# Other homes for the working tiles of an RWKV merge

## Chip, cores and metric

One core of a Trainium2 chip. The metric is the time of one execution on the device, in microseconds (us), as the median of several runs. The engines are TensorE (PE; its weight loads are listed as PEld), VectorE (DVE), ScalarE (ACT), GpSimd (POOL) and SyncE (SP), which issues the DMAs.

## The reference

Two layers of a diffusion backbone over 256 context and 256 latent tokens of 1024 channels. A layer is a half-step SwiGLU, a token mixing of three branches (retention, windowed attention, RWKV-7), and another half-step SwiGLU, all in float32. The change is in the RWKV branch, a recurrence over tokens in both directions, for 8 heads of 64 channels:

```python
# S_t = S_{t-1} (diag(w_t) - kk_t^T (a_t * kk_t)) + v_t^T k_t ;  y_t = S_t r_t
def step(S, inp):
    r_t, w_t, k_t, a_t, v_t, kk_t = inp
    sa = -jnp.einsum('bhvk,bhk->bhv', S, kk_t)
    S = (S * w_t[:, :, None, :] + sa[..., None] * (kk_t * a_t)[:, :, None, :]
         + v_t[..., None] * k_t[:, :, None, :])
    return S, jnp.einsum('bhvk,bhk->bhv', S, r_t)
...
ys_f, S_f = rwkv7_scan(r_s, *dirs_s[0], v_s, kk_s, zero_rw, False)
ys_b, S_b = rwkv7_scan(r_s, *dirs_s[1], v_s, kk_s, zero_rw, True)
yx_f, _ = rwkv7_scan(r_x, *dirs_x[0], v_x, kk_x, S_f, False)
yx_b, _ = rwkv7_scan(r_x, *dirs_x[1], v_x, kk_x, S_b, True)
```

The latent scans (x) start from the final state of the context scans (s). The second layer's output is wanted for the latent tokens alone.

## The kernel before

Channels lie on the 128 partitions, the 512 tokens (256 context, 256 latent) along the free dimension. Every dense product is three float32r matmuls (L186 to L188): the weights are loaded in blocks of four 128x128 tiles, ScalarE rounds them (L114) and VectorE takes the rest (L115).

In a mixing stage the string ORDER[l] gives the order in which the work of the branches is written down, by hand. The final order on each engine is made from it by a planner at build time, which runs a model of the machine with durations of its own, lets instructions whose inputs and buffers are there go ahead of others, and keeps in force how many tiles of each tag may be alive. A tile is asked for with mk(shape, tag, bufs): tiles of one tag share bufs homes, and a tile waits until one of them has been released by its last reader. PSUM banks are asked for with ps(tag); the tag "rx" has two.

RWKV is done for four pairs of heads p, and for the two streams, context (s = 0) and latent (s = 1), in chunks of 64 tokens. In ORDER, "A" and "C" are the fronts of context and latent, "B" and "D" their backs; "lo" makes the inputs of the low-rank products, "c" the columns of a pair.

- The front, rw_prep (L902 on), makes the decays, the keys and the products inside a chunk, with eight tiles of the tag "rt", and has GpSimd invert triangular blocks of 32 (L1008, L1009). The inverses go to the HBM tile td.
- The back is rw_merge, rw_vals, rw_chain and, where the output is wanted, rw_out. rw_merge loads the inverses (z, L1018), copies them into tg (L1026, L1027), transposes half of them into tn (L1023), and joins the blocks of 32 to blocks of 64 by two groups of small matmuls (L1035, L1040) with the copy xm (L1036) between them. rw_vals puts the values into ve, the tile in which the chain later replaces half of the rows by corrected values (L1088), and into the block-diagonal vbd (L1060). rw_chain goes through four chunks in both directions, 8 steps of some six short operations each, which wait for each other on TensorE, ScalarE and VectorE (L1079 to L1113); its result ya and the squares of rw_out take "rb" tiles.

Before the change tn, xm, ya and the squares share three homes of "rb"; ve has two homes, one for each direction; vbd is one lasting buffer, a slice of the constant tile cst; the "lo" inputs have three homes.

Of the kernel before, what the change touches and what calls it, by code (L numbers as in the profile page):

```python
# [18 lines left out]
CONSTS = {"ident": 0, "nw": 128, "adab": 176, "ones": 320, "bones": 384, "cm": 512, "mg": 640, "ks": 896, "all": 960}  # L19
# [103 lines left out]
def body(nc, tc, I, O, es, dbg=None):  # L123
# [3 lines left out]
    V, A, G, PE, SP = nc.vector, nc.scalar, nc.gpsimd, nc.tensor, nc.sync  # L127

    def mk(shape, tag, bufs=1, dt=F32):
        return sb.tile(shape, dt, name=tag, tag=tag, bufs=bufs)  # L130
# [3 lines left out]
    def ps(tag):  # L134
        return pp.tile([128, 512], F32, name="ps_" + tag, tag=tag, bufs=NB[tag])
# [13 lines left out]
    def span(S):  # L149
        return slice(S[0] * 256, S[-1] * 256 + 256)  # L150


    cst = mk([128, CONSTS["all"] + 1696 + 4360], "cst")
    n0 = CONSTS["bones"]
    SP.dma_start(out=cst[:, 0:n0], in_=I["cst"][:, 0:n0])
    SP.dma_start(out=cst[:, n0:CONSTS["all"]], in_=I["cst"][:, n0:])
# [1 line left out]
    def const(name, n):  # L158
        return cst[:, CONSTS[name]:CONSTS[name] + n]
# [4 lines left out]
    per = cst[:, CONSTS["all"]:]  # L164
# [3 lines left out]
    def sm(n, key, bufs=8):  # L168

        if key not in rings:  # L170
            rings[key] = [rings["at"], 0, n]
            rings["at"] += n * bufs
            assert rings["at"] <= CONSTS["all"] + 1696 + 4360
        r = rings[key]
        assert r[2] == n
        j = r[0] + n * (r[1] % bufs)
        r[1] += 1
        return cst[:, j:j + n]
# [1 line left out]
    hall = mk([128, KT, 2, 512], "hall", 1, F32R)  # L180
    hs = [(hall[:, kt, 0], hall[:, kt, 1]) for kt in range(KT)]

    rings = {"at": CONSTS["all"] + 1696}

    def mm3(o, w, h, start, stop):
        PE.matmul(o, w[0], h[0], start=start, stop=False)  # L186
# [19 lines left out]
    st = {"apart": False}  # L206
# [120 lines left out]
    def hl(h, c):  # L327
        return h[0][:, c], h[1][:, c]
# [21 lines left out]
    def first(W, key, H, cs, os, lead=0, lag=0):  # L350

        bl, n = W.take(key), len(os)
        w = {}
        parts = [(0, slice(0, 512))] if lead == 0 else [(0, CS[0]), (lead, CS[1])]
        for i in range(KT + lead + lag):
            for d, part in parts:
                k = i - d
                for j, (o, c) in enumerate(zip(os, cs)):
                    p = slice(max(c.start, part.start), min(c.stop, part.stop))
                    if 0 <= k < KT and p.start < p.stop:  # L360
                        if (k, j) not in w:
                            w[k, j] = W.get(bl[k * n + j])
                        for q in range(2):
                            PE.matmul(o[:, p], w[k, j][q], hl(H[k], p)[0], start=(k == 0 and q == 0 and p.start == c.start), stop=False)  # L364
                k -= lag
                for j, (o, c) in enumerate(zip(os, cs)):
                    p = slice(max(c.start, part.start), min(c.stop, part.stop))
                    if 0 <= k < KT and p.start < p.stop:
                        PE.matmul(o[:, p], w[k, j][0], hl(H[k], p)[1], start=False, stop=(k == KT - 1 and p.stop == c.stop))
# [424 lines left out]
    def conv(o, ct, c, st, dst):  # L794
        w = st["vec"][:, ct * 3:ct * 3 + 3]
        A.activation(dst[:, c], o[:, c], AF.Copy, scale=w[:, 1:2])
        n = (c.stop - c.start) // 256
        d = dst[:, c].rearrange("p (s t) -> p s t", s=n)
        s = o[:, c].rearrange("p (s t) -> p s t", s=n)
        V.scalar_tensor_tensor(d[:, :, 1:256], s[:, :, 0:255], w[:, 0:1], d[:, :, 1:256], ALU.mult, ALU.add)  # L800
        V.scalar_tensor_tensor(d[:, :, 0:255], s[:, :, 1:256], w[:, 2:3], d[:, :, 0:255], ALU.mult, ALU.add)  # L801

    def rw_consts():
        V.memset(per[:, 288:1312], 0.0)
        ub = per[:, 288:800].rearrange("p (d b x) -> p d b x", d=2, b=2)
        return dict(bones=const("bones", 128), cm=const("cm", 128), mg=const("mg", 256).rearrange("p (d x) -> p d x", d=2),
                    one=const("ones", 64), ks=const("ks", 1), ub=[[ub[:, d, b] for b in range(2)] for d in range(2)],
                    vbd=per[:, 800:1312].rearrange("p (q x) -> p q x", q=4))

    def rw_lora(W, H, l, S, st):  # L810
        full = slice(0, 512)
        vec = st["vec"]
        lo = []
        cs, os = (full, full, span(S)), [ps(t) for t in ("mm", "mm", "ap")]
        first(W, "lo", H, cs, os, 1, 1)
        for j, (c, o) in enumerate(zip(cs, os)):
            t = mk([128, 512], "lo", 3)
            conv(o, 12 + j, c, st, t)
            lo.append(t)
        c = span(S)  # L820
        A.activation(lo[0], lo[0], AF.Tanh)
        A.activation(lo[2][:, c], lo[2][:, c], AF.Tanh, scale=0.5)
        V.tensor_scalar(lo[2][:, c], lo[2][:, c], 0.5, 0.5, ALU.mult, ALU.add)
        st["sg"] = lo[2]
        st["lw"] = [[mk([128, 512], "lw", 4, F32R) for d in range(2)] for x in range(2)]
        for x in range(2):
            for d in range(2):
                hs, ot = (slice(64 * y, 64 * y + 64) for y in (d, 1 - d))
                A.copy(st["lw"][x][d][hs], lo[x][hs])
                V.tensor_sub(st["lw"][x][d][ot], lo[x][hs], st["lw"][x][d][hs].bitcast(F32))  # L830
        if l > 0:
            bl = W.take("vd")
            o = ps("mm")
            wh, wl = W.get(bl[0], 2)
            for kt in range(KT):
                ksl = slice(kt * 32, kt * 32 + 32)
                mm3(o[0:32], (wh[:, ksl], wl[:, ksl]), hl(H[kt], full), kt == 0, kt == KT - 1)
            vd = mk([128, 512], "vd")[0:32]
            A.copy(vd, o[0:32])
            st["vd"] = vd  # L840
# [172 lines left out]
        X["td"] = td  # L1013

    def rw_merge(X, st):
        z, tn, xm = mk([64, 2, 8, 32], "z", 2), mk([32, 16, 32], "rb", 3)[:, 0:8], mk([64, 16, 32], "rb", 3)[:, 0:8]
        for b in range(2):
            mark = SP.dma_start(out=z[32 * b:32 * b + 32].rearrange("p d u t -> p (d u) t"), in_=X["td"][16 * b:16 * b + 16].rearrange("u j g i -> (j g) u i")).ins  # L1018
        st["marks"].append(mark)
        fl = lambda t: t.rearrange("p u t -> p (u t)")  # L1020
        tg = X["tg"]
        tu = [tg[d].rearrange("p h c t -> p (h c) t") for d in range(2)]
        V.transpose(fl(tn), fl(z[0:32, 0]))  # L1023
        for b in range(2):
            bs = slice(32 * b, 32 * b + 32)
            A.copy(tu[0][bs, :, bs], z[bs, 0])  # L1026
            V.transpose(tu[1][bs, :, bs], z[bs, 1])  # L1027

        o = ps("rx")
        ov, o2 = (o[:, j * 256:j * 256 + 256].rearrange("p (u x) -> p u x", x=32) for j in range(2))  # L1030
        ab = (slice(0, 32), slice(32, 64))
        for d in range(2):
            a, b = ab[d], ab[1 - d]
            for u in range(8):
                PE.matmul(ov[b, u], X["off"][a, u], tn[:, u] if d == 0 else z[a, 1, u], start=True, stop=True)  # L1035
        A.copy(xm, ov[0:64])  # L1036
        for d in range(2):
            a, b = ab[d], ab[1 - d]
            for u in range(8):
                PE.matmul(o2[a, u], xm[b, u], tu[d][b, u, b], start=True, stop=True)  # L1040
        V.tensor_copy(tu[0][ab[0], :, ab[1]], o2[ab[0]])
        A.copy(tu[1][ab[1], :, ab[0]], o2[ab[1]])

    def rw_vals(s, R, st, want_y, X):
        c = CS[s]
        v = R["v"]

        ve = [mk([128, 4, 128], "ve", 2) for _ in range(2)]
        vb = st["vbd"]
        o = ps("rx")  # L1050
        for q in range(2):
            PE.matmul(o[:, q * 128:q * 128 + 128], v[:, c.start + q * 128:c.start + q * 128 + 128], st["cm"], start=True, stop=True)
        ov = o[:, 0:256].rearrange("p (c d) -> p c d", c=2)
        for a in range(2):
            rows = slice(64 * a, 64 * a + 64)
            for d in range(2):
                A.copy(ve[d][0:64, a::2], ov[rows])
            for h in range(2):
                hs = slice(64 * h, 64 * h + 64)
                A.copy(vb[hs, a::2, hs], ov[rows, :, hs])  # L1060
        X["ve"], X["vb"] = ve, vb
        if want_y:
            o = ps("rx")
            PE.matmul(o[:, 0:256], st["bones"], X["t"][:, 0], start=True, stop=True)
            bv = sm(256, "bv", 2)
            V.tensor_tensor(bv, o[:, 0:256], v[:, c], ALU.mult)
            X["bv"] = bv
# [159 lines left out]
    for l in range(2):  # L1227
# [17 lines left out]
        if not RC:  # L1245
            RC.update(rw_consts())
# [120 lines left out]
```

## Time and profile before

| what | us |
|---|---|
| median of three runs | 2946.3 (2938.15 to 2952.78) |
| the profiled execution's own time | 2950.47 |
| its span, first to last instruction | 2948.7 |
| TensorE busy | 2797.0 (95%) |
| VectorE busy | 2002.5 (68%) |
| ScalarE busy | 1319.8 (45%) |
| GpSimd busy | 376.2 (13%) |

The profile comes from one execution. Its times count from the span's start. Layer 0's mixing stage lies between about 410 and 1300 us, layer 1's between about 2070 and 2750 us. The granted clock is the share of its full speed that TensorE was given; it has two levels, 1.2 and 2.4 GHz, so a mean of 0.82 in a stretch says that about a third of it was at the lower one.

### The profile page before, as it was taken

The numbers are of one execution on the slowest core, as the hardware profiler recorded it, in microseconds if no ns is written. First come the engines' busy times: TensorE is split into PE (matmuls) and PEld (weight loads), VectorE is DVE, ScalarE is ACT, GpSimd is POOL, SyncE is SP. The second block draws the span as 40 slices with busy tenths as digits, with TensorE's granted clock in tenths as the row PEclk, the third lists the DMA queues.
The fourth block names the chain that finished last, engine by engine and source line by source line (L and its number), as shares of the span: only waits on it lengthen the run. The fifth ranks groups of instructions, "written<-read, shape, count | busy, mean of one in ns | idle before, by whom it ended". The sixth has DMA issues, their size and how long they took to land. (4 is left out here: it accounts for less than half of the span.)

```text
span 2948.7 us, 47410 instructions
## 1 busy us (share of the span) xinstructions
PE 2797.0 (95%) x16761; PEld 2389.1 (81%) x16761; DVE 2002.5 (68%) x4677; ACT 1319.8 (45%) x2968; POOL 376.2 (13%) x1068
## 2 busy tenths in 40 slices
PE   7999999889999999999999999999989889899999
PEld 6888888767877787788888888888878788788999
DVE  7977668676676666566756466465787767678655
ACT  3322245556555654333223232233567665565544
POOL 0000000522132112000000000000033434330000
PEclk9999999789999999999999999999999888899999
DMA  7655534212333136534534435343433234246554
GB/s 267 232 189 183 163 122 130 83 39 82 111 97 89 49 123 207 176 102 147 195 114 169 147 111 185 104 164 122 137 90 108 75 110 116 61 124 212 170 179 154
DMA packets 259727, 400.97 MB, mean 136 GB/s; under 512 B 78752, under 2 KB 96288, under 8 KB 259488
## 3 DMA queue, kind: packets, MB, share of 16 engines
q1 hardware_dynamic: 259488, 397.93, 42.2%
q8 instruction: 132, 2.16, 0.3%
q14 instruction: 107, 0.88, 0.1%
HBM read 368.33 MB, written 25.82 MB: 134 GB/s over the span
## 5 line engine op out<-in xcount | busy, mean ns | idle before, releaser
L114 ACT CAST whi<-raw 128x512 fp32r<-128x512 f32 x954 | 564.1, 618 | 675.7 <-PE ps_mm L187 350.0
L186 PE MATMUL ps_mm<-hall,whi 128*128 128x512 f32 (+1 forms) x2320 | 845.1, 365 | 10.2 <-DVE rr_v L801 4.0
L188 PE MATMUL ps_mm<-hall,wlo 128*128 128x512 f32 (+1 forms) x2320 | 842.6, 364 | 2.0 <-DVE wlo L115 2.0
L187 PE MATMUL ps_mm<-hall,whi 128*128 128x512 f32 (+1 forms) x2320 | 840.8, 363 | 0.0
L115 DVE TENSOR_TENSOR wlo<-raw,whi 128x512 fp32r<-128x512 f32 x954 | 643.8, 691 | 104.3 <-ACT whi L114 68.3
L186 PEld LDWEIGHTS ps_mm<-hall,whi 128*128 128x128 f32 x2320 | 442.9, 191 | 80.6 <-ACT cst L981 4.4
L188 PEld LDWEIGHTS ps_mm<-hall,wlo 128*128 128x128 f32 x2320 | 441.6, 191 | 74.8 <-DVE wlo L115 4.1
L187 PEld LDWEIGHTS ps_mm<-hall,whi 128*128 128x128 f32 x2320 | 442.0, 191 | 71.4 <-issue 0.2
L186 PE MATMUL ps_mm<-hid,whi 128*128 128x512 f32 (+1 forms) x737 | 260.6, 354 | 0.0
L187 PE MATMUL ps_mm<-hid,whi 128*128 128x512 f32 (+1 forms) x737 | 259.9, 354 | 0.0
L188 PE MATMUL ps_mm<-hid,wlo 128*128 128x512 f32 (+1 forms) x737 | 257.3, 354 | 0.0
L1008 POOL TENSOR_TENSOR cst<-acc,cst 128x60 f32<-128x60 f32 (+24 forms) x496 | 172.4, 348 | 615.5 <-DMA acc<-ad__10934 59.2
L401 DVE TENSOR_TENSOR ft<-ft,ps_mm 128x512 f32<-128x512 f32 (+1 forms) x80 | 49.7, 621 | 210.4 <-PE ps_mm L188 198.1
L373 DVE SCALAR_TENSOR_TENSOR x<-ps_mm,cst,x 128x256 f32<-128x256 f32 x136 | 61.0, 480 | 193.1 <-PE ps_mm L188 193.1
L853 POOL TENSOR_TENSOR ll<-lora,lh 128x512 fp32r<-128x512 f32 x8 | 10.3, 1282 | 1359.2 <-DVE ft L300 942.6
L1009 POOL TENSOR_TENSOR cst<-cst 128x60 f32<-128x60 f32 (+24 forms) x496 | 176.2, 355 | 38.1
L236 DVE SCALAR_TENSOR_TENSOR ft<-m,cd 128x1024 bf16<-128x1024 f32 x136 | 163.0, 1221 | 9.8 <-DMA m<-ada 9.8
L237 DVE SCALAR_TENSOR_TENSOR m<-m,cd 128x1024 f32<-128x1024 f32 x136 | 165.4, 1221 | 0.7
L186 PEld LDWEIGHTS ps_mm<-hid,whi 128*128 128x128 f32 x737 | 139.1, 189 | 19.6
L187 PEld LDWEIGHTS ps_mm<-hid,whi 128*128 128x128 f32 x737 | 139.1, 189 | 19.4
L188 PEld LDWEIGHTS ps_mm<-hid,wlo 128*128 128x128 f32 x737 | 138.5, 189 | 19.4
L187 PE MATMUL ps_mm<-wlo,hall 128*128 128x256 f32 x416 | 122.6, 295 | 2.7 <-DVE wlo L115 2.6
(339 smaller groups left out, 4505.3 us busy)
## 6 DMA issues: line engine op xcount, KB each, us to landing
m<-ada SPq DMA_DIRECT2D x136, 512.0 KB, 4.4
raw<-w0b SPq DMA_DIRECT2D x214, 256.0 KB, 2.9
raw<-w1b SPq DMA_DIRECT2D x211, 256.0 KB, 3.2
raw<-w0a SPq DMA_DIRECT2D x132, 256.0 KB, 2.8
raw<-w0c SPq DMA_DIRECT2D x132, 256.0 KB, 4.5
raw<-w1a SPq DMA_DIRECT2D x132, 256.0 KB, 4.3
raw<-w1c SPq DMA_DIRECT2D x132, 256.0 KB, 3.9
gd<-ft SPq DMA_DIRECT2D x24, 256.0 KB, 2.0
```

The lines of the kernel that those rows point to most:

```text
L114: nc.scalar.copy(hi, raw)
L115: nc.vector.tensor_sub(lo, raw, hi.bitcast(F32))
L186: PE.matmul(o, w[0], h[0], start=start, stop=False)
L187: PE.matmul(o, w[0], h[1], start=False, stop=False)
L188: PE.matmul(o, w[1], h[0], start=False, stop=stop)
L236: V.scalar_tensor_tensor(junk, raw, 1.0, st["cond"][0], ALU.mult, ALU.mult, accum_out=md[:, kt, 0:1])
L237: V.scalar_tensor_tensor(raw, raw, 1.0, st["cond"][1], ALU.mult, ALU.mult, accum_out=md[:, kt, 1:2])
L373: V.scalar_tensor_tensor(xs[n][:, CS[s]], o[:, CS[s]], gate[:, n, s:s + 1], xs[n][:, CS[s]], ALU.mult, ALU.add)
L401: V.tensor_tensor(sg[:, c], sg[:, c], pu[:, c], ALU.mult)
L853: G.tensor_sub(ll, lw, lh.bitcast(F32))
L1008: G.tensor_tensor(w, acc[j // 16][:, j % 16, j + 1:32].unsqueeze(1).to_broadcast([128, m, n]), tt[:, 0:m, j:j + 1].to_broadcast([128, m, n ...
L1009: G.tensor_tensor(tt[:, 0:m, j + 1:32], tt[:, 0:m, j + 1:32], w, ALU.add)
```

## The change

The two working tiles of a merge, tn and xm, are taken from "rt" (eight homes, those of the preparation) in place of "rb" (three homes, which stay). ve gets four homes in place of two; the first two "lo" inputs, which are dead long before, use them too, and "lo" keeps one home. vbd becomes two lasting buffers, one for each stream; the tile cst is 512 columns (2 KiB a partition) wider for it, and the second buffer is set to zero once. The PSUM banks, ORDER and all computing instructions but that memset stay as they were.

```diff
-    cst = mk([128, CONSTS["all"] + 1696 + 4360], "cst")
+    cst = mk([128, CONSTS["all"] + 2208 + 4360], "cst")
...
-    rings = {"at": CONSTS["all"] + 1696}
+    rings = {"at": CONSTS["all"] + 2208}
...
     def rw_consts():
         V.memset(per[:, 288:1312], 0.0)
+        V.memset(per[:, 1696:2208], 0.0)
...
-                    vbd=per[:, 800:1312].rearrange("p (q x) -> p q x", q=4))
+                    vbd=[per[:, a:a + 512].rearrange("p (q x) -> p q x", q=4) for a in (800, 1696)])
...
     def rw_lora(W, H, l, S, st):
...
-            t = mk([128, 512], "lo", 3)
+            t = mk([128, 512], "ve", 4) if j < 2 else mk([128, 512], "lo")
...
     def rw_merge(X, st):
-        z, tn, xm = mk([64, 2, 8, 32], "z", 2), mk([32, 16, 32], "rb", 3)[:, 0:8], mk([64, 16, 32], "rb", 3)[:, 0:8]
+        z, tn, xm = mk([64, 2, 8, 32], "z", 2), mk([32, 16, 32], "rt", 8)[:, 0:8], mk([64, 16, 32], "rt", 8)[:, 0:8]
...
     def rw_vals(s, R, st, want_y, X):
...
-        ve = [mk([128, 4, 128], "ve", 2) for _ in range(2)]
-        vb = st["vbd"]
+        ve = [mk([128, 4, 128], "ve", 4) for _ in range(2)]
+        vb = st["vbd"][s]
```

## Rows read from the trace of the kernel before

**Rows 1.** The page: busy time of the engines, and the granted clock in 40 slices.

```profile
PE 2797.0 (95%) x16761; PEld 2389.1 (81%) x16761; DVE 2002.5 (68%) x4677; ACT 1319.8 (45%) x2968; POOL 376.2 (13%) x1068
...
PEclk9999999789999999999999999999999888899999
```

**Rows 2.** Waits of TensorE: what waited, for what, us in total, times, longest.

```profile
PE ps_rx L1035 <- DVE rb L1023: 10.3, 3, 7.6
...
PE ps_rf L957 <- DVE kb L946: 6.2, 5, 2.3
...
PE ps_rx L1079 <- DVE rb L1113: 5.0, 5, 2.2
```

**Rows 3.** VectorE in order of time, merges of layer 0: D0, D2 and B3.

```profile
603.17 0.98 DVE L1027 STREAM_TRANSPOSE tg<-z 32x256 f32<-32x256 f32 x2
...
609.83 0.43 DVE L1023 STREAM_TRANSPOSE rb<-z 32x256 f32<-32x256 f32 x1
...
955.47 0.90 DVE L1027 STREAM_TRANSPOSE tg<-z 32x256 f32<-32x256 f32 x2 [4.12 <-DMA z<-td]
...
989.39 0.42 DVE L1023 STREAM_TRANSPOSE rb<-z 32x256 f32<-32x256 f32 x1
...
1051.90 0.43 DVE L1027 STREAM_TRANSPOSE tg<-z 32x256 f32<-32x256 f32 x1 [4.59 <-DMA z<-td]
1052.27 0.39 DVE L1023 STREAM_TRANSPOSE rb<-z 32x256 f32<-32x256 f32 x1
```

**Rows 4.** Busy time by stretches of layer 0: from one chain to the next.

```profile
609.00:634.00 25.00, 20.83 (x148) 16.91 (x148) 15.16 (x55) 11.27 (x32) 0.00 (x0) 0.82 0.04 11
702.00:723.00 21.00, 18.48 (x147) 14.25 (x147) 14.71 (x45) 14.09 (x42) 0.00 (x0) 0.84 0.13 36
782.00:808.00 26.00, 26.00 (x183) 21.35 (x182) 20.04 (x63) 17.81 (x45) 1.11 (x3) 1.00 0.31 107
882.00:907.00 25.00, 23.21 (x152) 18.05 (x151) 12.58 (x35) 11.93 (x30) 0.00 (x0) 0.82 0.26 87
987.00:1007.00 20.00, 17.53 (x133) 14.44 (x132) 11.96 (x39) 12.21 (x37) 0.00 (x0) 0.75 0.11 33
1156.00:1182.00 26.00, 25.72 (x176) 20.81 (x174) 22.13 (x47) 13.86 (x30) 0.00 (x0) 1.00 0.91 318
sum 143.00, PE 131.78 PEld 105.81 DVE 96.58 ACT 81.15 POOL 1.11; mean PE 21.96 PEld 17.63 DVE 16.10 ACT 13.53 POOL 0.19
```

The columns are the stretch, its length, the busy time (with the count of instructions) of PE, PEld, DVE, ACT and POOL, the granted clock, the DMA share and GB/s.

**Rows 5.** The same for the eight other stretches of layer 0, 634 to 1232.

```profile
634.00:702.00 68.00, 63.41 (x402) 52.99 (x400) 46.76 (x116) 38.61 (x94) 23.46 (x67) 0.95 0.34 99
...
808.00:882.00 74.00, 67.21 (x442) 57.61 (x440) 57.95 (x153) 38.80 (x91) 26.07 (x66) 0.99 0.35 100
...
sum 480.00, PE 456.45 PEld 375.37 DVE 314.97 ACT 242.92 POOL 131.76; mean PE 57.06 PEld 46.92 DVE 39.37 ACT 30.36 POOL 16.47
```

The six stretches left out there have a granted clock of 1.00.

**Rows 6.** TensorE, and once VectorE, in order of time, where merges wait for z.

```profile
558.08 0.90 PE L1035 MATMUL ps_rx<-rb,cst 32*32 32x32 f32 x13 [7.57 <-DVE rb L1023]
```

```profile
2197.86 0.56 PE L1035 MATMUL ps_rx<-rb,cst 32*32 32x32 f32 x13 [1.56 <-DVE rb L1023]
...
2383.65 0.56 PE L1035 MATMUL ps_rx<-rb,cst 32*32 32x32 f32 x13 [1.19 <-DVE rb L1023]
...
2518.47 0.66 PE L1079 MATMUL ps_rx<-cst,gk 128*64 128x128 f32 x2 [5.79 <-DVE cst L1102]
```

```profile
2516.52 0.43 DVE L1023 STREAM_TRANSPOSE rb<-z 32x256 f32<-32x256 f32 x1 [7.35 <-DMA z<-td]
```

**Rows 7.** Busy time in three more stretches: around layer 0's first merge, and layer 1.

```profile
553.00:577.00 24.00, 18.32 (x128) 16.81 (x129) 12.43 (x51) 10.04 (x33) 7.92 (x25) 0.51 0.37 102
2453.00:2481.00 28.00, 27.54 (x186) 22.89 (x186) 21.42 (x61) 14.94 (x38) 0.00 (x0) 0.79 0.27 77
2533.00:2541.00 8.00, 7.33 (x97) 5.83 (x98) 2.56 (x7) 7.08 (x24) 0.00 (x0) 1.00 0.05 18
```

**Rows 8.** Single lines: ns min/median/max, first and last start in us, shapes.

```profile
L1057 ACT COPY ve<-ps_rx x64: 356/368/372, 561.0 to 2655.2; 64x256 f32<-64x256 f32 x64
```

```profile
L1060 ACT COPY cst<-ps_rx x64: 257/262/272, 561.5 to 2655.7; 64x128 f32<-64x128 f32 x64
```

```profile
L804 DVE MEMSET cst<- x1: 912/912/912, 1.0 to 1.0; 128x1024 f32 x1
```

More of the change, by code (lines that the diff above doesn't have):

```diff
@@ L172, in sm @@
             rings["at"] += n * bufs
-            assert rings["at"] <= CONSTS["all"] + 1696 + 4360
+            assert rings["at"] <= CONSTS["all"] + 2208 + 4360
         r = rings[key]
```

## The prediction

> **What bounds the kernel now.** I read the page's first two parts first, then TensorE's waits, then the traffic of one RWKV merge on VectorE, then the busy time by stretches of layer 0's mixing stage. TensorE is busy for 95% of the span, and the clock line dips only in the two mixing stages [rows 1]. So no other engine bounds the kernel as a whole, and a change of buffers can win only what TensorE loses there: time in which it stands idle, and time in which it runs at half clock (1.2 instead of 2.4 GHz). I count both: in a stretch of length T the idle loss is T minus TensorE's busy time, and the clock loss is T times (1 minus the granted clock), since at half clock half of the columns of that time are missing. The second is a little generous where TensorE waits for latency and not for columns.
>
> Where do the homes that the change touches bind? For each pair of heads and each stream the merge waits for the DMA that brings z, copies z into tg (L1026, L1027), transposes it into tn (L1023), and two groups of matmuls with the copy xm between them follow. L1027 and L1023 need the same z. In layer 0 they are apart: for the first D0 merge 603.17 and 609.83, for D2 955.47 and 989.39, only for B3 1051.90 and 1052.27 [rows 3]. Six of layer 0's eight merges start tn late by 6.7 to 34 us, although z is there. By the code this is the wait for a home: tn and xm come out of the same three "rb" homes as the chain's result ya and rw_out's squares, so they follow the rw_out of the stream before. Behind tn, rw_vals then waits too, because ve and vbd are still read by the chain. So the chain of one stream stops, and a merge and the copies of the values go by before the next chain starts: 20 to 26 us each time.
>
> What do these six transitions cost? They are the six stretches of [rows 4]: 143 us, TensorE busy 131.78, so 11.2 us idle; the clock loss is 25 x 0.18 + 21 x 0.16 + 25 x 0.18 + 20 x 0.25 = 17.4 us. Together 28.6 us, 20% of the time. The eight stretches between and after them, where the chains run (in one of them the z of B3 is awaited), are 480 us with 23.6 us idle and 3.4 + 0.7 = 4.1 us of clock loss [rows 5]: 27.7 us, 5.8%.
>
> **The change part by part.** *tn and xm from "rt".* The merge of the next stream no longer waits for rw_out. It keeps its instructions, and it is placed beside the chain before it. If the transitions then lose only at the rate of the stretches where chains run, 5.8% of 143 us is 8.3 us, and 28.6 - 8.3 = 20.3 us come back. That is the gain that I take; the bounds are 0 (the loss only moves with the merge) and 28.6 us (it goes altogether).
>
> *What is late next.* A merge that starts when z lands waits for z in the middle of the work, and TensorE keeps its order: behind the merge's first matmul stand the dense matmuls. The trace has ten prompt merges: B0 and B3 of layer 0 and the eight of layer 1. TensorE stood idle behind z for 7.57 us at B0, and in layer 1 for 1.56, 1.19 and 5.79 us (the last at the chain's L1079, behind a VectorE that sat 7.35 us until z) [rows 6]. The other six show no such gap; TensorE's waits list only three behind L1023 [rows 2]. That is 16.1 us for ten, 1.6 us each. Six more prompt merges cost 9.7 us. The bounds are 0 for all six and, for one of them, what B0 lost in all: in the 24 us around it TensorE is busy 18.3 us at a granted clock of 0.51, so 5.7 + 11.8 = 17.4 us [rows 7].
>
> *Does "rt" have the room?* The preparation asks for eight rt tiles, but its first ones (ts, L) are dead before the last two (dg, dr) are written, so I take it that two places are free whenever a merge runs: cost 0. If they are not, the preparation is held up, and TensorE meets that at L957; what it loses there now is 6.2 us in all [rows 2], so the bounds are 0 and another 6.2.
>
> *Four homes of ve, two of vbd.* The values' matmuls and eight copies of ScalarE (four of 368 ns and four of 262 ns, so 2.5 us per stream [rows 8]) can go before the chain ahead of them has ended. Same count, another place: 0 by themselves; they are part of the 20.3 us, since without them the next chain would wait here instead. In layer 1 they matter at two places, where z was there before the chain ahead had ended: 28 us with 0.5 us idle and 5.9 us of clock loss, and 8 us with 0.7 us idle [rows 7], 7.0 us in all. I take 0 of it, because the clock loss there is around the merge itself, which stays prompt; the bound is 7.0. Layer 1's other transitions wait for z, and the change does nothing to POOL's inverse or its DMAs.
>
> *The small parts.* One memset of 512 columns more: the one of 1024 took 912 ns at 1.0 us of the span [rows 8], so about 0.46 us of VectorE at the start, while TensorE waits for weights: 0. The "lo" tiles of the low-rank inputs borrow two homes of ve; they are dead before the first chain: 0. The one lasting buffer is 2 KiB a partition larger, and ve can hold 4 KiB more at a time. No view shows how full the memory is; I put that with the rt term (0 to 6.2 us, taken as 0).
>
> The sum: -20.3 + 9.7 = -10.6 us, on the profiled execution of 2950.5 us (its span 2948.7 and 1.8 us around it): 2939.9 us. That execution is 4.2 us above the median of the three runs, 2946.3 us; against the median the same 10.6 us give **2936 us**.
>
> A rule speaks for more. The Trainium skill, "Perfetto Trace Analysis", Optimization Strategy, says that a gap which recurs on the engine that ought to be saturated can mean that there is no room for the next tile, and names buffer counts. By that rule the transitions' loss would belong wholly to the missing homes, and the time would be that of the second case below. The trace agrees that a home is waited for at six merges, but it also shows losses around merges that had their homes in layer 1, so I don't follow the rule to its end.
>
> **The ways in which it could go.**
> *First: the transitions shrink, and prompt merges take half of it back.* 2936 us, from 2926 (merges cost nothing) to 2942 (the rt bound is paid). Chance 0.40. For it: the losses per stretch above. Against it: the order of the instructions is made anew by a planner from modelled times, and each stall after this comes where that plan is wrong about the chip.
>
> *Second: all of it comes back.* The chains follow each other without a break, and the next z has time to land while the last chain runs. -28.6 - 7.0 = -35.6 us: 2911 us. For it: at B3, the prompt merge of layer 0 in the middle of the run, TensorE lost nothing. Against it: layer 1 loses as much with its prompt merges. Chance 0.26.
>
> *Third: the change does not do what it says.* Merge, values and chain share two PSUM banks ("rx"). A chain step holds one until its result is added at L1113, and TensorE has waited for that already, 5.0 us in five places [rows 2]. A merge that runs beside a chain takes one of the two banks, the chain is longer by what the transition is shorter, and TensorE's losses stay: 2946 us, within 5 us. Against it: bank time is idle in the transitions. Chance 0.10.
>
> *Fourth, slower: z's landing becomes TensorE's wait.* Place: the first merge matmuls (L1035) of D0, B1, D1, B2, D2 and D3 in layer 0. Now the late homes hide z from TensorE; without them it joins ScalarE and VectorE, which wait for z already (L1026, L1027) with the conversions of the weights (L114, L115) queued behind. If two of the six behave as B0 and four as the mean: 2 x 17.4 + 4 x 1.6 - 20.3 = +20.9 us, 2967 us. It decides for slower by over 0.5% once the six cost (20.3 + 14.7) / 6 = 5.8 us each. For it: B0. Against it: none of the eight in layer 1 cost as much. That all six do (+84 us) I leave out for that reason. Chance 0.24.
> The Trainium skill, "TensorE: Matmul & The Clock Gate", in its architectural detail, says that ScalarE's and VectorE's queues are strictly first in, first out. By it a merge issued early would hold every conversion behind it, and the time would be the fourth case's. The trace agrees in kind: VectorE sat 7.35 us until z before L1023.
>
> **How the numbers follow.** A measurement of this kernel can tell about 0.5%, 14.7 us, from no change (its three runs lie 14.6 us apart): faster is under 2931.6, slower over 2961. Of the first case I count 0.12 as faster and 0.28 as the same; with the second, faster is 0.38. The same is 0.28 + 0.10 = 0.38. Slower is 0.24. The range for 8 in 10 goes from a little under the second case to a little over the fourth, 2908 to 2968 us; the first case's own is 2926 to 2942.
>
> **What would show it.** Right: L1023 within 2 us of L1027 at all of layer 0's merges; the chain (L1079) of the next stream within some 10 us of the end of the one before; layer 0's six transitions losing under 10 us together; L1035 waiting behind L1023 for some 15 to 25 us in all instead of 10.3. Wrong: L1023 still late (the homes were not what held it: third case), a half-clock stretch of 10 us or more at each new prompt merge (fourth), waits of the preparation's ScalarE and VectorE work on rt tiles, or gains and losses far from RWKV, in the attention or the branches, which would mean that the new order as a whole weighs more than the homes.

## The result: slower, and outside the range

The changed kernel takes 2974.15 us (median of four runs, 2970.36 to 2975.69) against 2947.78 us of the kernel before beside it: 1.0092 of its time, 95% interval 1.0064 to 1.0119. The profiled span is 2973.0 us against 2948.7. From the memset on, each line number is higher by one: L1023 is now L1024, L1035 L1036, L1036 L1037, L1134 L1135, L910 L911.

Page of the changed kernel, busy time and granted clock:

```profile
PE 2805.0 (94%) x16761; PEld 2398.3 (81%) x16761; DVE 1993.1 (67%) x4678; ACT 1307.0 (44%) x2968; POOL 369.6 (12%) x1068
...
PEclk9999999887998999999999999999999799899999
```

The clock line dips in the same two stages as before [rows 1]: in layer 0 in four slices instead of two, in layer 1 in two instead of four. Busy time of the two mixing stages, first of the kernel before, then of the changed one (columns as in [rows 4]):

```profile
404.00:1310.00 906.00, 846.87 (x5190) 703.90 (x5188) 618.15 (x1621) 467.60 (x1133) 183.84 (x532) 0.95 0.35 108
2063.00:2747.00 684.00, 622.84 (x4697) 551.04 (x4696) 505.17 (x1358) 411.97 (x1036) 192.15 (x532) 0.93 0.39 117
```

```profile
401.00:1327.00 926.00, 852.69 (x5195) 711.52 (x5194) 614.31 (x1622) 460.99 (x1133) 180.20 (x532) 0.93 0.35 105
2079.00:2772.00 693.00, 627.32 (x4700) 554.81 (x4699) 503.28 (x1359) 409.51 (x1033) 189.19 (x532) 0.91 0.41 120
```

Layer 0's stage is 19 us longer (925.3 us, before 905.9) and layer 1's 9 (692.8, before 684.1); the rest of the span is 4 us shorter. TensorE is idle there for 73.3 + 65.7 = 139.0 us instead of 59.1 + 61.2 = 120.3, and its granted clock is lower by 0.02 in both. TensorE's waits in the changed kernel (for what; us in total, times, longest):

```profile
PE ps_rx L1135 <- DVE rb L1132: 23.2, 6, 8.9
PE ps_rf L958 <- DVE kb L947: 15.4, 9, 5.9
...
PE ps_rx L1036 <- DVE rt L1024: 7.9, 4, 4.1
...
PE ps_rx L1080 <- DVE rb L1114: 2.4, 3, 1.4
```

The merge's wait for its own transpose fell, from 10.3 to 7.9 us, and the chain's for its bank from 5.0 to 2.4; the preparation's rose from 6.2 to 15.4 [rows 2]. The first line is new among the large ones: the wait of rw_out's sums for its squares after they are normalised on VectorE (5.7 us, three times, before). At D0 of layer 0, VectorE and then TensorE in order of time:

```profile
597.51 0.43 DVE L1024 STREAM_TRANSPOSE rt<-z 32x256 f32<-32x256 f32 x1 [3.41 <-DMA z<-td]
597.88 0.39 DVE L1028 STREAM_TRANSPOSE tg<-z 32x256 f32<-32x256 f32 x1
598.30 0.68 DVE L1127 TENSOR_REDUCE cst<-rb 64x8 f32<-64x512 f32 x1
...
601.47 0.69 DVE L1132 TENSOR_TENSOR rb<-rb,cst 64x512 f32<-64x512 f32 x1
```

```profile
602.31 0.66 PE L1135 MATMUL ps_rx<-cst,rb 64*128 64x64 f32 x4 [8.86 <-DVE rb L1132]
604.05 0.90 PE L1036 MATMUL ps_rx<-rt,cst 32*32 32x32 f32 x13
```

tn is prompt now, 0.4 us from L1028 instead of 6.7 behind it [rows 3]. But VectorE stands at it for 3.41 us until z lands, with the squares' sum (L1127) of the output before behind it; TensorE waits 8.86 us for that output (3.08 us at the same place before), and the merge's matmuls come behind the output's all the same. The same picture, VectorE at L1024 for 5.53 and 3.47 us, is ahead of two more of the six waits (5.83 and 3.59 us): 18.3 of the 23.2 us. In layer 0 alone the waits of this kind rise from 4.3 to 16.8 us. But tn is not prompt everywhere: at B1, D1, D2 and B3 of layer 0 it is 3, 8, 19 and 38 us behind L1028, and B3's was prompt before [rows 3]. VectorE at B3:

```profile
1061.87 0.90 DVE L1028 STREAM_TRANSPOSE tg<-z 32x256 f32<-32x256 f32 x2 [8.25 <-DMA z<-td]
...
1100.36 0.39 DVE L1024 STREAM_TRANSPOSE rt<-z 32x256 f32<-32x256 f32 x1
```

The six transitions of [rows 4], each from the squares of an output to the next chain:

```profile
594.00:619.00 25.00, 16.69 (x126) 13.80 (x127) 15.26 (x50) 9.34 (x24) 0.00 (x0) 0.65 0.20 50
690.00:728.00 38.00, 29.20 (x186) 24.25 (x187) 22.26 (x62) 18.95 (x52) 11.40 (x35) 0.69 0.09 23
790.00:812.00 22.00, 22.00 (x164) 17.91 (x163) 10.96 (x33) 10.34 (x26) 0.00 (x0) 1.00 0.38 115
881.00:908.00 27.00, 21.18 (x143) 17.74 (x142) 11.48 (x32) 8.86 (x23) 4.18 (x14) 0.75 0.26 62
984.00:1023.00 39.00, 32.83 (x240) 26.55 (x239) 25.30 (x78) 24.51 (x64) 3.63 (x15) 0.91 0.13 35
1168.00:1192.00 24.00, 22.85 (x148) 17.73 (x147) 17.11 (x37) 12.13 (x27) 0.00 (x0) 0.93 0.88 306
sum 175.00, PE 144.75 PEld 117.97 DVE 102.38 ACT 84.12 POOL 19.22; mean PE 24.12 PEld 19.66 DVE 17.06 ACT 14.02 POOL 3.20
```

They are 175 us instead of 143, with 30.3 us idle instead of 11.2; the clock loss, by the prediction's measure, is 32.5 us instead of 17.4. Last, ScalarE at the same place:

```profile
605.85 0.37 ACT L1037 COPY rt<-ps_rx 64x256 f32<-64x256 f32 x1 [0.66 <-ACT ft L472]
606.12 0.47 ACT L911 ACTIVATE rt<-ps_rf,cst 128x256 f32<-128x256 f32 x1
```

The first tile of the next preparation (A1, L911) is written right behind the merge's xm; its matmuls were done at 581. Before, L910 of A1 ran at 583.

### The profile page after: what moved, and what is told of

Same layout as the page of the kernel before. It is cut to its first block, busy times and chain, and to the rows that moved or that the text cites. A ratio compares the mean times of both kernels' runs of the same rounds, so it can differ in the third digit from the quotient of the medians.

```text
span 2973.0 us, 47539 instructions
## 1 busy us (share of the span) xinstructions
PE 2805.0 (94%) x16761; PEld 2398.3 (81%) x16761; DVE 1993.1 (67%) x4678; ACT 1307.0 (44%) x2968; POOL 369.6 (12%) x1068
## 5 line engine op out<-in xcount | busy, mean ns | idle before, releaser
L210 ACT CAST hid<-ft 128x512 fp32r<-128x512 f32 (+1 forms) x88 | 49.9, 568 | 255.8 <-DVE ft L401 255.7
L186 PEld LDWEIGHTS ps_mm<-hid,whi 128*128 128x128 f32 x737 | 139.0, 189 | 19.6
L187 PEld LDWEIGHTS ps_mm<-hid,whi 128*128 128x128 f32 x737 | 139.0, 189 | 19.6
```

Of the source, the lines that this page charges most:

```text
L187: PE.matmul(o, w[0], h[1], start=False, stop=False)
L210: A.copy(dst[0], src)
```

## The experiments

**ORDER**: the planner lets a tag's tiles, and a PSUM tag's banks, be written first in the order in which the program asks for them (tiles asked for in one line aside), however many homes there are. tn followed the squares of the output before because those are asked for before it, in rb; in rt, the preparations written after a merge follow its xm, and GpSimd's inverse and z come later. The built programs say the same: of the 16 tn before, the first write of 11 is made to follow L1123 and of 4 the xm of the merge before; with rt, the first rt tile of 6 of the 16 preparations is made to follow an xm (A1, A2, C2 and C3 in layer 0, A2 and A3 in layer 1). With five homes of rb the program is that of the kernel before, instruction for instruction, and with ten of rt that of the changed kernel. **HOMES**: the counts bind. **Z**: early merges stall TensorE on z. **MEMORY**: the larger tiles crowd out others. **QUEUE** (from e13 on): the prompt transposes hold VectorE until z, with the normalisation of the output before behind them.

The stages are measured from their first L283 to the next stage's, in the one profiled execution of each run; "before" is 905.9 and 684.1 us. e2 and e7 have the same computing instructions in the same order, but for one memset, and differ by 9 us in layer 0 and 3 in layer 1: a difference of that size between two stages shows nothing by itself. The time and the ratio come from all executions of a run.

| run | edit | us | ratio (95%) | layer 0 | layer 1 |
|---|---|---|---|---|---|
| the change | | 2974.15 | 1.0092 (1.0064 to 1.0119) | 925.3 | 692.8 |
| e1 | tn, xm in rt | 2979.68 | 1.0106 (1.0079 to 1.0132) | 911.3 | 709.1 |
| e2 | ve 4, vbd 2 | 2939.18 | 0.9961 (0.9944 to 0.9977) | 907.2 | 683.2 |
| e3 | tn, xm in lasting columns | 2952.33 | 1.0012 (0.9994 to 1.0029) | 920.6 | 675.5 |
| e4 | tn in rt | 2964.86 | 1.0051 (1.0034 to 1.0069) | 915.0 | 693.9 |
| e5 | tn, xm in a tag of their own | 2957.77 | 1.0032 (1.0017 to 1.0046) | 915.1 | 680.5 |
| e6 | merge's bank from rf | 2996.52 | 1.0159 (1.0140 to 1.0179) | 925.6 | 712.3 |
| e7 | 512 unused columns | 2939.57 | 0.9964 (0.9950 to 0.9978) | 898.4 | 680.5 |
| e8 | e1, preparations written earlier | 2956.73 | 1.0023 (1.0005 to 1.0041) | 900.6 | 705.4 |
| e9 | rw_out written later | 2967.62 | 1.0076 (1.0058 to 1.0095) | 923.6 | 685.0 |
| e10 | e9 and e5 | 2958.54 | 1.0048 (1.0032 to 1.0063) | 911.8 | 689.4 |
| e11 | e9 and e7 | 2959.24 | 1.0046 (1.0026 to 1.0066) | 923.3 | 687.5 |
| e12 | as e9, ahead of the values | 2957.71 | 1.0038 (1.0023 to 1.0052) | 921.2 | 674.9 |
| e13 | the change, held | 2945.15 | 0.9984 (0.9968 to 1.0001) | 880.4 | 709.6 |
| e14 | e5, held | 2924.58 | 0.9919 (0.9894 to 0.9944) | 884.7 | 682.7 |
| e15 | e2, held | 2947.05 | 1.0001 (0.9988 to 1.0015) | 898.9 | 684.7 |
| e16 | before, held | 2926.14 | 0.9918 (0.9897 to 0.9939) | 881.8 | 685.2 |
| e17 | e13, rt in layer 0 alone | 2925.05 | 0.9908 (0.9892 to 0.9925) | 888.0 | 682.3 |
| e18 | e1, held | 2964.61 | 1.0052 (1.0034 to 1.0069) | 903.8 | 702.4 |

### The parts of the change: e1, e2, e7

```diff
# e1
-        z, tn, xm = ..., mk([32, 16, 32], "rb", 3)[:, 0:8], mk([64, 16, 32], "rb", 3)[:, 0:8]
+        z, tn, xm = ..., mk([32, 16, 32], "rt", 8)[:, 0:8], mk([64, 16, 32], "rt", 8)[:, 0:8]
# e2: the change, but for that line
# e7
-    cst = mk([128, CONSTS["all"] + 1696 + 4360], "cst")
+    cst = mk([128, CONSTS["all"] + 2208 + 4360], "cst")
```

> The kernel before with one edit: tn and xm come from rt; ve, vbd and the memory stay. Theory ORDER (the homes of a tag are handed out in the order in which the program asks for them, so a preparation written after a merge gets its rt tiles only when that merge has taken tn and xm): slower than before by 20 to 35 us, as the changed kernel (+27), with the first ScalarE step of a preparation (L910) right behind the merge's L1036. Rival MEMORY (the 2 KiB and the two more ve homes crowd out other tiles): within 8 us of before. Rival Z (prompt merges make TensorE wait for z): slower by 20 to 30 us, with the loss behind L1035.

> The other half: ve with four homes, vbd twice, 2 KiB more of lasting memory; tn and xm stay in rb. ORDER: within 12 us of before, and the values' copies are no earlier against the chain ahead, because their banks (rx) are handed out behind that chain's. MEMORY: slower by 20 to 30 us. Z: within 8 us of before.

> The kernel before with nothing but 512 unused columns more in cst (2 KiB a partition). The planner makes of it the order of the second experiment. ORDER: the homes of ve and vbd do nothing, so the time of the second experiment: 0.996 of before, within 0.3%. If two homes of ve and vbd save waits on the chip itself: between before and 0.998, slower than the second experiment. MEMORY: slower than before.

The one line of tn and xm is the whole loss: +1.06% alone. It does not lie in the same place, though: e1 loses 5 us in layer 0 and 25 in layer 1, the change 19 and 9. The homes of ve and vbd do nothing: e2's gain of 0.4% is e7's, which only makes the constant tile wider, and the two have the same order of computing instructions. e7 also says what a plan is worth by chance: an edit that no instruction uses moves the time by 0.4%. ScalarE in e1, where the preparation follows xm as in the changed kernel:

```profile
607.24 0.36 ACT L1036 COPY rt<-ps_rx 64x256 f32<-64x256 f32 x1 [0.67 <-PE ps_rx L1035]
607.50 0.47 ACT L910 ACTIVATE rt<-ps_rf,cst 128x256 f32<-128x256 f32 x1
```

### Other homes for tn and xm: e3, e4, e5

```diff
# e3, with 512 more columns of cst as in the change
+        tn, xm = (per[0:n, a:a + 256].rearrange("p (u t) -> p u t", t=32) for n, a in ((32, 1696), (64, 1952)))
# e4: tn from "rt", 8, xm stays in "rb"
# e5
+        z, tn, xm = ..., mk([32, 16, 32], "mw", 2)[:, 0:8], mk([64, 16, 32], "mw", 2)[:, 0:8]
```

> tn and xm get lasting places of their own, 2 x 256 columns of cst, so that they stand in no tag's queue; all else as before (ve two homes, vbd one). ORDER: preparations as early as before; between 12 us faster and 8 us slower than before. MEMORY (the same 2 KiB): slower by 20 to 30 us. Z (tn is as prompt as in the changed kernel): slower by 20 to 30 us.

> Only tn comes from rt; xm stays in rb, memory as before. ORDER: a preparation is held only until z has landed and not until the merge's first matmuls are through, so slower by 5 to 20 us, less than with both. Z: the full 20 to 30 us, since tn is what waits for z. MEMORY: within 8 us of before.

> The first experiment with one word changed: tn and xm come from a tag of their own with two homes in place of rt; no lasting memory is added, ve and vbd as before. The merges have what the change gave them, and no preparation shares their queue. ORDER: the loss of the first experiment (+31 us) goes; between 12 us faster and 8 us slower than before, with L910 of a preparation no longer behind L1036 of a merge. Z (prompt merges cost): still slower by 20 to 30 us. MEMORY: not in play; within 8 us.

e5 differs from e1 in the tag alone (one that nothing else uses, with two homes), and takes 22 us less. Its preparation is early again while the merge still follows the output (ScalarE, then TensorE):

```profile
577.93 0.48 ACT L910 ACTIVATE rt<-ps_rf,cst 128x256 f32<-128x256 f32 x1 [0.68 <-PE ps_rf L909]
```

```profile
608.62 0.43 PE L1134 MATMUL ps_rx<-cst,rb 64*128 64x64 f32 x4 [2.92 <-DVE rb L1131]
610.13 0.90 PE L1035 MATMUL ps_rx<-mw,cst 32*32 32x32 f32 x13
```

In e4 the preparation follows tn (L1023 at 598.45, L910 at 599.50). All as ORDER has it; but e5 stays 9.5 us above the kernel before, where only tn moved, a little beyond ORDER's bound. That was left open until e14. Z's 20 to 30 us are not there: in e3 tn is within 1 us of its L1028 at every merge, and the time is that of the kernel before within the interval.

### The bank, and the written order: e6, e8

```diff
# e6, in rw_merge
-        o = ps("rx")
+        o = ps("rf")
# e8, on e1: in ORDER
-... kv c1 D0 H0 H1 q0 A1 ... D1 A2 G3 q1 B2 P2 G4 C2 ...
+... kv c1 A1 D0 H0 H1 q0 ... A2 D1 G3 q1 C2 B2 P2 G4 ...
# and in layer 1 A1 ahead of D0, A2 of D1, A3 of D2
```

> The kernel before, with the PSUM bank of a merge asked for under rf (the preparation's one bank) and no longer under rx; tn and xm in rb as before. ORDER, if it holds for banks too: merges no longer come after the rw_out ahead of them (L1035 before L1134), but every matmul of a preparation written after a merge comes after that merge's L1042; slower than before by 25 to 60 us. If banks are handed out as they come free: merges and preparations mix freely, and it is within 15 us of before.

> The first experiment (tn and xm from rt, nothing else), with fronts written ahead of merges in ORDER: A1 before D0, A2 before D1, C2 before B2 in layer 0; c1 and A1 before D0, A2 before D1, A3 before D2 in layer 1. ORDER: now the merges stand behind those preparations in rt's queue: tn (L1023) of D0 comes right after A1's last rt tile is first written (L980), no preparation comes right after L1036, and the time is within 20 us of before, to either side, since a late merge costs as a late preparation does. Were it room and not order, both would go on as in the first experiment, at +31 us.

Without the bank of rx, the merge's matmuls go ahead of the output's, and the preparation's (L908, also rf) now follow the merge (TensorE in e6):

```profile
600.86 0.87 PE L1035 MATMUL ps_rf<-rb,cst 32*32 32x32 f32 x13 [2.11 <-DVE rb L1023]
...
604.66 0.68 PE L1134 MATMUL ps_rx<-cst,rb 64*128 64x64 f32 x4
607.00 0.56 PE L908 MATMUL ps_rf<-lw,lh 128*128 128x256 f32 x1
```

So it was the order of rx that held the merge, and the price for changing it was 48 us. In e8 the preparations stand ahead of the merges, and tn now waits until the last tile of a preparation is written (by L989, where the expectation named L980). VectorE; it had copied all of z by 602:

```profile
618.76 0.44 DVE L989 STREAM_TRANSPOSE rt<-rt 64x256 f32<-64x256 f32 x1 [2.38 <-PE ps_mm L188]
619.23 0.43 DVE L1023 STREAM_TRANSPOSE rt<-z 32x256 f32<-32x256 f32 x1
```

### rw_out written later: e9 to e12

The edit, abridged:

```diff
     def rw_back(l, p, s, S, st):
         rw_merge(X[s], st)
         rw_vals(s, R, st, s in S, X[s])
+        flush(st)  # writes the output that is still owed; e12: ahead of rw_vals
         ya = rw_chain(l, p, s, R, st, s in S, s == 0, X[s])
         if s in S:
-            rw_out(l, p, s, R, st, ya, X[s])
+            st["out"] = out  # rw_out and its DMA; also written ahead of the next "c"
```

> The kernel before, with tiles and banks as there; only rw_out is written later: behind the merge and the values of the next stream with a back, in place of right behind its own chain. ORDER: the merge's bank of rx and its two rb homes are now asked for ahead of rw_out's, so L1035 of D1, B2, D2, D3 and their like comes ahead of the normalisation matmuls of the output before (its squares and its sums), and the stretch from one chain to the next is shorter by what rw_out takes there, some 3 to 10 us each; the preparation's rt tiles are where they were. Time from -25 to +5 us against the kernel before. Z (an early merge stalls TensorE on the inverses): 10 to 30 us slower. HOMES (three rb homes are too few): no change of the places, within 5 us.

> The run before, and tn and xm in a tag of their own with two homes. ORDER: the squares of rw_out no longer stand behind tn and xm in rb, otherwise the same places; within 10 us of the run before, on either side. HOMES: now at last tn has a home of its own and the merge its place: 10 to 30 us faster than the kernel before.

> The late rw_out, and the 512 columns of the constant tile that nothing uses (they made the kernel before 0.4% faster by the plan that the smaller memory makes). ORDER: the same places as in the late rw_out alone; if the two add up, 10 us less than that run; the other plans differ by -0.4% to +0.3% for edits that touch nothing, so no more than that is expected to hold.

> The late rw_out once more, but written between the merge and the values of the next stream. ORDER: L1035 still ahead of the output's sums, as the merge is written first; the values' banks (L1057, L1060) now follow rw_out's, so the next chain begins about as late as in the kernel before: time within 10 us of it. Z: as slow as the late rw_out, since the merge is as early in both.

The places are ORDER's without an exception, but two that the expectation names were wrong: ahead of D0, D1 and D2 stands a "c", so the output is written before them as ever. L1035 follows L1134 at D0, D1 and D2 (e9: 649.17 and 650.19; 834.25 and 835.27) and is ahead of it at B1, B2, B3 and D3 (725.31 and 740.37 at B1). In e12 the values' copies of B1 move behind the output (L1057 at 740.51, in e9 at 728.56). The times miss: all four are slower than before, by 11 to 21 us, where 25 us less to 5 more were expected of e9. A merge that is early in full wins nothing here. The gaps between layer 0's chains (from a chain's last L1107 to the next one's first L1079) and the chains themselves show where it goes: before 200 and 465 us, in e10 172 and 497, in e1 177 and 494. In these two the chains gain what the gaps lose. In e16 below they do not: its gaps are 175 us, its chains 466, and layer 0's stage is 24 us shorter.

### Transposes held behind the normalisation: e13 to e18

```diff
     # in rw_out
-        V.tensor_tensor(sq, y, ..., ALU.mult)
+        st["nm"] = V.tensor_tensor(sq, y, ..., ALU.mult).ins
     # in rw_merge
+        with tc.issue_after(st["nm"]) if "nm" in st else nullcontext():
             V.transpose(fl(tn), fl(z[0:32, 0]))
             ...
     # e17 also
+        g = ("rb", 3) if st["l"] else ("rt", 8)
```

> The changed kernel, with VectorE's transposes of a merge (tn and tg) queued behind the normalisation of the output before them (rw_out's last product on VectorE); tiles and banks as changed. QUEUE (the prompt transposes wait for z on VectorE with that normalisation behind them, and TensorE then waits for it): TensorE's wait for the normalised squares falls from 23.2 to under 8 us, and the time by 10 to 20 us against the changed kernel, to 2954 to 2965 us; what ORDER costs by the later preparations stays. ORDER alone: that wait costs nothing in the end, 2966 to 2980 us.

> The kernel before with tn and xm in homes of their own, and the transposes of a merge queued behind the normalisation of the output before. QUEUE: the 9.5 us that the homes of their own cost are the prompt transposes' wait, so they go: 0.997 to 1.001 of the kernel before. ORDER alone: tn is now where it is in the kernel before and nothing else is, so 1.000 as well; only if those 9.5 us are the chance of one plan does it stay at 1.002 to 1.005.

> Four homes for ve and two vbd, tn and xm in rb (0.996 of the kernel before), and the transposes queued behind the normalisation; tn is there already, so only the transposes into tg move. QUEUE: 0.992 to 0.996, as VectorE's waits for z ahead of the normalisation go. ORDER alone: 0.994 to 0.998, no wait of TensorE changes by more than 3 us.

> The kernel before with the transposes queued behind the normalisation. As in the run with four homes for ve: QUEUE 0.995 to 0.999, ORDER alone 0.998 to 1.002.

> The changed kernel with held transposes, and tn and xm in rt in layer 0 alone; in layer 1 they stay in rb. ORDER and QUEUE, each in its place: layer 0's mixing stage as in the changed kernel with held transposes (about 880 us, against 905.9 before), layer 1's as in the kernel before (about 684 us, against 709.6 with rt and held transposes): 2915 to 2930 us, 0.990 to 0.994 of the kernel before. If the two stages' lengths are the chance of single plans: anything from 2920 to 2960 us.

> tn and xm in rt, everything else as before (2979.7 us, 1.0106), with held transposes. QUEUE in layer 0: its stage falls from 911 us to 880 to 890. ORDER in layer 1: its stage stays at 705 to 712 us, since the preparations still follow the merges' xm. Together 2940 to 2955 us, 0.998 to 1.003 of the kernel before.

This only orders VectorE's queue: the transposes of a merge (tn and tg) come behind the last product of the output written before. In the changed kernel it takes 29 us away, more than expected. Busy time of its two mixing stages with held transposes (e13), its wait for the squares (under 8 us was expected), and the two stages of the kernel before with held transposes (e16):

```profile
402.00:1283.00 881.00, 828.49 (x5194) 692.69 (x5194) 614.87 (x1622) 461.12 (x1133) 179.79 (x532) 0.97 0.36 110
2037.00:2746.00 709.00, 635.02 (x4692) 562.96 (x4692) 501.95 (x1358) 408.07 (x1033) 195.61 (x532) 0.90 0.40 118
```

```profile
PE ps_rx L1136 <- DVE rb L1133: 8.9, 2, 4.9
```

```profile
403.00:1284.00 881.00, 834.04 (x5181) 695.27 (x5181) 615.37 (x1621) 462.33 (x1134) 184.80 (x532) 0.96 0.37 111
2037.00:2722.00 685.00, 620.74 (x4697) 551.37 (x4696) 502.63 (x1359) 412.25 (x1034) 189.79 (x532) 0.93 0.39 117
```

Layer 0's stage falls by 45 us, to the length that the kernel before has with the same edit (881.8): in this plan rt costs nothing there. Layer 1's does not fall; it gets 17 us longer. As the kernel before gains 21.5 us by the same edit, the 29 us do not undo the change: with held transposes in both, it is still 19 us slower (e13 and e16), and that is in layer 1, whose stage is 24 us longer. Of the five kernels that got the edit, layer 0 is shorter in all (before by 24, e5 30, e2 8, the change 45, e1 8 us; the 8 us are within what one program differs by), and homes of their own stop costing (e14 as e16). QUEUE is right on the side, and too small in size, in e13 and e16. In e16 VectorE's idle time until z (L1023 and L1027 together) falls from 51.0 to 23.0 us, but TensorE's wait for the normalised squares, which is all that QUEUE names, only from 5.7 to 3.7: how the other gain reaches TensorE was not followed. QUEUE is wrong for e15, which lost the 0.4% of e2 instead of gaining, and I have no cause for that. e17 came out as the two causes together say; it is as fast as e14 and e16, which have no tile in rt, within the intervals. e18 has layer 1 near what was expected, layer 0 14 us above it (22 above e16), and misses its range.

Layer 1 sorts the runs by one thing. With both tiles in rt it takes 692.8, 709.1, 709.6 and 702.4 us (the change, e1, e13, e18); with neither, in the eight runs that leave banks and written order alone (e2, e3, e5, e7, e14 to e17), 675.5 to 685.2. z of B1 is issued 287 us after the stage's start in the changed kernel and 291 in e1, against 261 before and 254 in e5. With tn alone in rt it takes 693.9 (e4). ORDER's cost is there: 9 us in the change, 18 to 26 in the others. Late preparations are not the whole of it: in e8 none follows an xm and z of B1 is issued at 261 us, yet layer 1 takes 705.4 us; there six merges have tn 13 to 49 us behind L1027. The cost is measured, not followed to the last us: idle time and half clock rise together, over the whole stage.

## Why the prediction was wrong

- **What bounds the kernel**: TensorE, in the two mixing stages, by idle time and clock. That held: both stages grew, by both losses.
- **"By the code this is the wait for a home"**: the step that failed first. The rows showed that tn comes right behind the squares; that it waits for the squares' *place in the order*, not for a free home, was not to be seen in the number of homes, and the program with five homes is the same. From it came the third part's cost, and a sign that I had named, L1023 still late: tn is late at four of layer 0's merges, now behind preparations.
- **"Does rt have the room?", 0 (bound 6.2 us at L957)**: the question was wrong. There was room (ten homes give the same program); the order was the price. L958's wait alone rose by 9.2 us, and layer 1 pays 9 us here and 18 to 26 us in the three other kernels with both tiles in rt.
- **The gain, -20.3 us**: did not come; the six transitions lose 62.7 us by the measure that gave 28.6. The merge's matmuls stayed behind the output's, by the order of rx (e6, e9). Where gaps between chains did shrink with earlier merges (e1, e10), the chains grew by as much. A gain of that size in layer 0 (24 us) came the other way round, with the output first and the merge's transposes behind it (e16).
- **The merges' wait, +9.7 us**: the mechanism was right, its place was not. (Its count was a little off too: in layer 1 two of the eight merges called prompt had tn 2.8 and 5.3 us behind L1027, at D0 and B2.) I sized it at L1035, which now waits less than before. It sits on VectorE, where I named only weight conversions as queued behind; the output's normalisation is queued there too, and TensorE's wait for it rose from 5.7 to 23.2 us. Held, layer 0 loses its 19 us and 25 more; the kernel before loses 24 there by the same edit. The fourth rival was nearest, 2967 us, with the slower sign and the right engine, at the wrong instruction. That its number comes near is luck: its sum prices waits at L1035, and those fell. Its rule of the Trainium skill ("TensorE: Matmul & The Clock Gate", architectural detail: VectorE's queue is strictly first in, first out) is what the rows at D0 show, 3.41 us there and 8.86 us on TensorE.
- **The second case** rested on the missing home. The rule beside it, that a recurring gap can mean a lack of room for the next tile (the Trainium skill, "Perfetto Trace Analysis", Optimization Strategy), does not hold for this gap: more homes change no instruction.
- **The third rival** named the two rx banks: right that they hold the merge, though by their order and not by their number (e6, e9), wrong that this leaves the time as it was.
- **ve and vbd, memset, lo, 0**: held; e2 is e7. The larger tile, which I put at a cost of 0 to 6.2 us, brought 0.4% (e7).

So the change costs 27 us by two things that both come from the tag. Sharing rt's order with the preparations costs 22 us against homes of their own (e1 and e5), and with held transposes 1.3% (e18 and e14). Prompt transposes on VectorE cost 9.5 us with homes of their own, which is no more than a plan's chance is worth (e7), and nothing once they are held (e5; e14 as e16). In the change's own stages the second shows in layer 0 and the first in layer 1. What stays open is the size of each within a stage: the same edit moves layer 0 by 8 to 45 us in different plans, and why rw_out written later costs time was not settled.

## What to carry to other kernels

Before more homes are given to a tile, ask whether the count binds at all: build with two homes more, and if the program stays the same, the tile waits for an order, and another tag means another queue and other tiles behind it. When an instruction that waits for a DMA moves forward on an engine, list everything that stands behind it on that engine, not only the work that the wait was hiding. And an early consumer is worth nothing where its engine has other work for the time: here it is better late, behind the output that TensorE wants (e16, 0.8% faster than before; e17 0.9%; of the five kernels that got the edit, e15 alone did not gain).

## What I had not expected

An edit that only widens a tile by 512 columns that nothing uses changed the time by 0.4%, as much as the homes that the change adds. And the fastest kernels came from *delaying* three short VectorE transposes per merge (0.39 to 0.43 us each at D0) by some microseconds: TensorE's idle time in layer 0's stage fell from 59.1 to 47.0 us (e16), and the granted clock rose from 0.95 to 0.96.
